# Issuing both column halves of the probability-value products behind one eviction, in a two-layer attention trunk

## The chip, the cores and the metric

The kernel is one program on one core of a Trainium2 chip. The metric is the device time of one execution in microseconds (us), the median over the timed runs. Before the change three runs took 1315.16, 1319.93 and 1320.21 us, so the median is 1319.93 us. Everything about where the time goes comes from one further execution that the hardware profiler recorded.

In the profile, PE is TensorE's matmuls, PEld its weight loads, DVE is VectorE, ACT is ScalarE, POOL is GpSimd and SP issues DMAs. A line number such as L1058 is a line of the kernel. Tile names are shown without their buffer numbers: `s_po` is a PSUM tile of the pool `po`.

## What is computed

The reference is a two-layer decoder trunk on one sequence of 512 tokens with 1024 features, in float32. Cut to what matters here:

```
layer 0: h = rmsnorm(x); q, k, v, gates = split(h @ a_w_in)
         o = gated sum of three attention branches (compressed, selected, window), 12 heads of 64, causal
         o_mem = attention of 4 heads over 256 memory tokens
         x = x + concat(o, o_mem) @ a_w_out;  x = x + relu(rmsnorm(x) @ w_up)^2 @ w_down
shared keys and values from x
layer 1: q = rmsnorm(x) @ b_w_in; dilated attention, 8 slots x 3 groups, over the shared keys and values
         o_mem as above;  x = x + concat(o, o_mem) @ b_w_out;  squared-ReLU MLP as above
```

Every attention branch ends in a product of probabilities and values, out = softmax(scores) @ v, with a head dimension of 64. These products are what the change touches.

## The kernel before

**The work.** The program runs through six stretches: a start with the first projection, the attention of layer 0 with its projections, the MLP of layer 0, the shared keys and values with the first projection of layer 1, the attention of layer 1, and the MLP of layer 1. The large projections and the MLPs are made of products of two-part numbers: `mm3` (L250) issues three matmuls for each product (L253, L254, L255).

**An item of attention** has a front and a back. The front multiplies queries and keys into a PSUM tile of the pool `ps`, takes the maximum on DVE, the exponential on ACT (recorded at L216) and scales on POOL (`pscale`, L684). The back transposes the probabilities on PE into a PSUM tile of the pool `pt` (L1039 and L1045 in layer 0, L1540 and L1549 in layer 1, L638 for the memory heads) and copies them to an SBUF tile with the tag `pt4`. This copy is called an eviction below. It is made by `evT` (L686), which gives it to DVE for some of the calls (L690) and to ACT for the rest (L692); in layer 1 all of them go to ACT. `attend` (L142) runs fronts and backs of the items with a lag of one and mixes in steps of projections that are due.

**The products of probabilities and values** come at the end of the last item of a group. Two heads share one PSUM tile `O` of the pool `po`, which has a single buffer: the first head writes the output partitions 0 to 63 and the second head 64 to 127. So each product is a matmul with only 64 columns of the array, and they are written in pairs, first head and second head in turn. Four places do this:

- L1058 in layer 0, 12 groups. Six of them (first half of the queries) have 4 pairs, with 256, 128, 256 and 128 moving columns; six (second half) have 8 pairs, for each of two branches 256, 256, 256 and 128.
- L646 for the memory heads, 4 groups of 2 pairs with 512 columns, two in layer 0 and two in layer 1.
- L1562 in layer 1, 4 groups of 4 pairs with 256, 256, 256 and 128 columns.
- L1575 in layer 1, 4 groups of 4 pairs with 128 columns.

That makes 24 groups and 224 such matmuls. Each is a float32 matmul and stands in the trace as two MATMUL records, so that a group of 4 pairs shows as x16. The first head's probabilities of a group are evicted well before the second head's; in the second half of the queries in layer 0, the two branches of the second head have an eviction each.

**What sets the order.** The program is built with a scheduler that decides the order of the instructions on each engine while the kernel is built, from its own idea of when operands are ready. On the chip each engine then takes its instructions in that fixed order, and an instruction waits on semaphores for what it needs. Since a matmul of the first head needs only the first head's evictions, the scheduler may place it ahead of its partner, with other work between the two.

Of the kernel before, what the change touches and what calls it, by code (L numbers as in the profile page):

```python
# [10 lines left out]
AF = mybir.ActivationFunctionType  # L11
# [169 lines left out]
class K:  # L181
# [428 lines left out]
    def mem_items(self, kf, qm, kk, outs, seg, need):  # L610

        nc = self.nc

        def front(h, ih):
            Sp = self.ps(self.pS, [P, 2, NMEM])
            for ii in range(2):
                i = ih * 2 + ii
                for hl in (0, 1):
                    nc.tensor.matmul(
                        Sp[:, ii, :], qm[0][h // 2][:, h % 2, i * P : (i + 1) * P], kk[0][hl][:, h, :],  # L620
                        start=hl == 0, stop=hl == 1,
                    )
            p, sm = self.soft(Sp, 2, NMEM)
            c = self.t("cr", [P, 2])
            nc.vector.reciprocal(out=c, in_=sm)
            for ii in range(2):
                self.pscale(p[:, ii, :], c[:, ii : ii + 1])
            return p

        pT = {}  # L630

        def back(h, ih, p):
            if ih == 0:
                pT[h] = self.t("pt4", [P, 2, S])
            pt = self.ps(self.pT, [P, 2, 2, P])
            for kb in range(2):
                for ii in range(2):
                    nc.tensor.transpose(pt[:, kb, ii, :], p[:, ii, kb * P : (kb + 1) * P], self.idf)  # L638
            self.evT(pT[h][:, :, ih * 256 : (ih + 1) * 256].rearrange("p k (i q) -> p k i q", q=P), pt)
            if h % 2 == 0 or ih == 0:  # L640
                return
            O = self.ps(self.pO, [P, S])
            for kb in range(2):
                for hp in range(2):
                    hh = h - 1 + hp
                    nc.tensor.matmul(  # L646
                        O[hp * 64 : hp * 64 + 64, :], kf[0][kb][1][:, hh * HD : (hh + 1) * HD], pT[hh][:, kb, :],
                        start=kb == 0, stop=kb == 1,
                    )
            oT = self.t("act", [P, 2, S], F32R)  # L650
            self.split(oT, O)
            outs.append(oT)

        return [Item(front, back, (h, ih), seg, need) for h in range(4) for ih in range(2)]

    def hilo(self, ki, src):
# [29 lines left out]
    def evT(self, dst, src):  # L686

        self.n += 1
        if self.n % self.ev == 0:
            self.nc.vector.tensor_copy(dst, src)  # L690
        else:
            self.nc.scalar.activation(dst, src, AF.Copy)  # L692

    def q_out(self, t, f, dsts, keys=None, e=None):

# [268 lines left out]
    def attn_a(self, g, ga, gt, cmp, out):  # L964


        nc = self.nc
# [58 lines left out]
        def back(pr, half, hp, ii, p):  # L1026
            v = ga[2]
            i = half * 2 + ii
# [25 lines left out]
            for br in range(2):  # L1054
                for j in range(nj):
                    o = P if j == nj - 1 else 0
                    for x in range(2):
                        nc.tensor.matmul(  # L1058
                            O[x * 64 : x * 64 + 64, q0 + o : q0 + 256], v[:, j, br, :], st[x][br][:, j, o:256],
                            start=half == 0 and br == 0 and j == 0, stop=False,  # L1060
                        )
# [5 lines left out]
        need = f"g{g}" if g else None  # L1067
        return (
            [Item(front, back, a, g, need) for a in order],
            [Item(cfront, cback, (i,), g, "cmp") for i in range(NB)],  # L1070
        )
# [397 lines left out]
    def attn_b(self, sp, q4, kv, oT, side):  # L1469

        nc = self.nc
# [84 lines left out]
        def close0():  # L1556
            vn = kv[1]
            O = self.ps(self.pO, [P, S])
            for j in (0, 2, 1, 3):
                n = min(2, NB - j) * P  # L1560
                for s in range(2):
                    nc.tensor.matmul(  # L1562
                        O[s * 64 : s * 64 + 64, j * P : j * P + n], vn[:, j, s * HD : (s + 1) * HD],
                        t0[s][:, j * 256 : j * 256 + n], start=j == 0, stop=j == NB - 1,
                    )
            a = self.t("raw", [P, S])
            nc.scalar.activation(a.rearrange("p (r u) -> p r u", r=4), self.perm(O), AF.Copy)
            acc.append(a)

        def close1():  # L1570
            vp = kv[2]
            O = self.ps(self.pO, [P, S])
            for r in range(4):
                for s in range(2):
                    nc.tensor.matmul(  # L1575
                        O[s * 64 : s * 64 + 64, r * P : (r + 1) * P], vp[:, r, s * HD : (s + 1) * HD], t1[s][:, r, :],
                        start=True, stop=True,
                    )
            side.add(self.norm_b(st0, st1, acc[0], O, oT))
# [184 lines left out]
```

## Time and profile before

| | us |
|---|---|
| median of three timed runs | 1319.93 |
| lowest and highest | 1315.16, 1320.21 |
| span of the profiled execution | 1316.2 |
| PE busy in it | 1266.8 |
| DVE, ACT, POOL busy | 860.7, 772.2, 377.6 |

The span runs from the first to the last instruction of the profiled execution. It is 3.7 us under the median of the timed runs and inside their spread. Ends of matmuls are modelled in the profile and reach a little into the next matmul, so how long a run of matmuls holds the array is read from starts: from its first start to the start of what comes next.

### The profile page before, as it was taken

What the parts mean: (1) busy time and instruction counts of PE and PEld (TensorE: products, weight loads), DVE (VectorE), ACT (ScalarE), POOL (GpSimd) and SP (SyncE); (2) the same over time, 40 slices, a digit from 0 to 9 for tenths busy, and PEclk for the clock granted to TensorE, in tenths of its full rate; (3) what the DMA queues carried; (4) which work ended last, traced back from release to release, by engine and by line L of the source; (5) the groups of instructions that cost most, each with busy time, mean ns of one, the idle gap of its engine ahead of it and who ended that gap; (6) DMA issues with size and microseconds to landing.
All of it is one profiled execution on the core that took longest, in us unless ns stands there. A gap on an engine that the chain in (4) does not pass through costs nothing.

```text
span 1316.2 us, 18557 instructions
## 1 busy us (share of the span) xinstructions
PE 1266.8 (96%) x6468; PEld 1041.7 (79%) x6468; DVE 860.7 (65%) x1597; ACT 772.2 (59%) x1699; POOL 377.6 (29%) x478
## 2 busy tenths in 40 slices
PE   9789989999999999999999989989999999999998
PEld 7768777677688888888887888877768888888887
DVE  6987767744566656566588566675665655747566
ACT  6765668674575354453557457777657545354462
POOL 4455574443240000000003679562324000000000
PEclk9899989999999999999999999999999999999999
DMA  7333222334379697796965431210338879697434
GB/s 263 120 98 106 97 97 81 63 74 113 120 245 240 219 279 219 262 247 208 290 197 165 134 79 49 67 45 9 95 120 267 232 269 225 221 280 223 154 112 160
DMA packets 61837, 215.28 MB, mean 164 GB/s; under 512 B 6736, under 2 KB 14928, under 8 KB 61232
## 3 DMA queue, kind: packets, MB, share of 16 engines
q1 hardware_dynamic: 50800, 143.72, 32.9%
q0 software_dynamic: 9344, 35.77, 13.8%
q10 hardware_dynamic: 1600, 34.61, 7.2%
q8 instruction: 51, 0.84, 0.2%
q14 instruction: 42, 0.34, 0.1%
HBM read 208.83 MB, written 72.35 MB: 214 GB/s over the span
## 4 chain that ended last, share of the span: by engine, by line
PE 81%; DVE 8%; ACT 4%; issue 2%; POOL 2%; DMA 2%; POOLq 0%; ACTq 0%; DVEq 0%
PE s_ps L253 13%; PE s_ps L254 13%; PE s_ps L255 13%; PE s_acc L253 6%; PE s_acc L254 6%; PE s_acc L255 6%; PE s_pt L253 3%; PE s_pt L254 3%; PE s_pt L255 3%; PE s_po L1058 2%; DVE s_w L248 2%; PE s_ps L1500 1%; PE s_pt L1045 1%; ACT s_p L216 1%; PE s_ps L1009 1%
## 5 line engine op out<-in xcount | busy, mean ns | idle before, releaser
L248 DVE TENSOR_TENSOR s_w<-s_st,s_w 128x1024 fp32r<-128x1024 f32 (+3 forms) x240 | 290.1, 1213 | 260.3 <-ACT s_w L246 259.8
L246 ACT ACTIVATE s_w<-s_st 128x1024 fp32r<-128x1024 f32 (+4 forms) x272 | 263.8, 973 | 188.0 <-PE s_pt L255 49.5
L253 PE MATMUL s_ps<-s_act,s_w 128*128 128x512 f32 x568 | 222.6, 394 | 1.4 <-ACT s_act L288 1.4
L254 PE MATMUL s_ps<-s_act,s_w 128*128 128x512 f32 x568 | 222.0, 391 | 0.0
L255 PE MATMUL s_ps<-s_act,s_w 128*128 128x512 f32 x568 | 221.8, 391 | 0.0
L253 PEld LDWEIGHTS s_ps<-s_act,s_w 128*128 128x128 f32 x568 | 106.8, 188 | 26.1 <-ACT s_act L288 3.1
L254 PEld LDWEIGHTS s_ps<-s_act,s_w 128*128 128x128 f32 x568 | 106.9, 188 | 22.9 <-issue 0.8
L255 PEld LDWEIGHTS s_ps<-s_act,s_w 128*128 128x128 f32 x568 | 106.9, 188 | 22.1
L253 PE MATMUL s_acc<-s_w,s_act 128*128 128x512 f32 (+3 forms) x288 | 103.8, 365 | 4.5 <-DVE s_tq L1424 2.6
L254 PE MATMUL s_acc<-s_w,s_act 128*128 128x512 f32 (+3 forms) x288 | 103.4, 361 | 2.2 <-DVE s_w L248 1.4
L216 ACT ACTIVATE s_p<-s_ps 128x512 f32<-128x512 f32 x64 | 38.2, 597 | 112.6 <-PE s_ps L255 112.6
L255 PE MATMUL s_acc<-s_w,s_act 128*128 128x512 f32 (+3 forms) x288 | 101.5, 358 | 0.0
L1128 POOL DMA_DIRECT2D sum<-in_w_db_dram x16 | 14.4, 902 | 300.0 <-ACT s_p L216 298.3
L684 POOL TENSOR_SCALAR s_p<-s_p,s_cr 128x256 f32<-128x256 f32 (+3 forms) x128 | 71.6, 581 | 73.3 <-DVE s_cr L1021 21.7
L216 ACT ACTIVATE s_p<-s_ps,s_nm 128x256 f32<-128x256 f32 (+3 forms) x128 | 65.6, 522 | 17.6 <-DVE s_nm L1000 7.5
L248 POOL TENSOR_TENSOR s_w<-s_st,s_w 128x512 fp32r<-128x512 f32 (+4 forms) x32 | 52.2, 1630 | 59.3 <-ACT s_w L246 59.2
L253 PEld LDWEIGHTS s_acc<-s_w,s_act 128*128 128x128 f32 x288 | 56.5, 196 | 12.5 <-DVE s_tq L1424 3.0
L692 ACT ACTIVATE s_pt<-s_pt 128x512 f32<-128x512 f32 (+2 forms) x97 | 50.7, 529 | 25.2 <-PE s_pt L638 12.1
L254 PEld LDWEIGHTS s_acc<-s_w,s_act 128*128 128x128 f32 x288 | 56.5, 196 | 7.3 <-DVE s_w L248 2.2
L255 PEld LDWEIGHTS s_acc<-s_w,s_act 128*128 128x128 f32 x288 | 56.3, 196 | 4.8 <-issue 0.6
L288 ACT ACTIVATE s_qk<-s_p 128x256 fp32r<-128x256 f32 (+1 forms) x96 | 46.9, 489 | 22.0 <-DVE s_p L1138 20.1
L1128 POOL DMA_DIRECT2D sum<-sum x16 | 14.1, 884 | 143.5 <-issue 45.8
(338 smaller groups left out, 2995.2 us busy)
## 6 DMA issues: line engine op xcount, KB each, us to landing
s_st<-in_w_up_dram SPq DMA_DIRECT2D x64, 512.0 KB, 4.3
s_st<-sum SPq DMA_DIRECT2D x64, 512.0 KB, 6.0
s_st<-in_w_db_dram SPq DMA_DIRECT2D x48, 512.0 KB, 4.3
sum<-in_w_db_dram POOLq DMA_DIRECT2D x16, 1024.0 KB, 13.5
sum<-sum POOLq DMA_DIRECT2D x16, 1024.0 KB, 9.8
s_st<-in_w_bq_dram SPq DMA_DIRECT2D x16, 384.0 KB, 3.2
s_st<-in_w_ag_dram SPq DMA_DIRECT2D x11, 512.0 KB, 4.5
s_st<-in_w_c_dram SPq DMA_DIRECT2D x8, 512.0 KB, 3.7
```

Of the source, the lines that this page charges most:

```text
L216: return lambda *a, **k: self.marks.append(f(*a, **k))
L246: nc.scalar.activation(w[:, 0], st, AF.Copy)
L248: e.tensor_tensor(out=w[:, 1], in0=st, in1=w[:, 0], op=ALU.subtract)
L253: mm(ps, lh[0], rh[0], start=start, stop=False, skip_group_check=again)
L254: mm(ps, lh[0], rh[1], start=False, stop=False, skip_group_check=again)
L255: mm(ps, lh[1], rh[0], start=False, stop=stop, skip_group_check=again)
L288: nc.scalar.activation(dst[:, 0], src, AF.Copy)
L684: self.nc.gpsimd.tensor_scalar(out=p, in0=p, scalar1=c, scalar2=1.0, op0=ALU.mult, op1=ALU.mult)
L692: self.nc.scalar.activation(dst, src, AF.Copy)
L1009: nc.tensor.matmul(Sp, q[:, blk], kk[hl][:, br, 0:n], start=hl == 0, stop=False)
L1058: nc.tensor.matmul(O[x * 64 : x * 64 + 64, q0 + o : q0 + 256], v[:, j, br, :], st[x][br][:, j, o:256], start=half == 0 and br == 0 and j = ...
L1128: self.behind(self.nc.gpsimd.dma_start(t[o], x, accum_op=ALU.add, max_dma_last_dim=4096))
```

## The change

`evT` keeps the eviction that it issued last in `self.turned`. A new helper `pair` issues a matmul and adds a dependency on that eviction, so that the matmul can't be placed or start before it. All four places that multiply probabilities by values call `pair` instead of `matmul`. When they are reached, the last eviction is that of the item that closes the group, which is the second head's last one. So both halves of every pair in a group depend on it, the first head's as well, and in the groups with 8 pairs also the pairs of the branch whose evictions were done earlier. Nothing else is edited. Matmuls and their sizes stay the same.

```
@@ evT
         self.n += 1
         if self.n % self.ev == 0:
-            self.nc.vector.tensor_copy(dst, src)
+            self.turned = self.nc.vector.tensor_copy(dst, src)
         else:
-            self.nc.scalar.activation(dst, src, AF.Copy)
+            self.turned = self.nc.scalar.activation(dst, src, AF.Copy)
+
+    def pair(self, *a, **k):
+
+        i = self.nc.tensor.matmul(*a, **k)
+        self.tc.add_manual_dep(
+            i.ins, self.turned.ins.name, mybir.DependencyInfo(mybir.DependencyClass.Sync, mybir.DependencyReason.DATA),
+            reason="both halves of the array together",
+        )
@@ attn_a, back (the same in mem_items, close0 and close1)
                     for x in range(2):
-                        nc.tensor.matmul(
+                        self.pair(
                             O[x * 64 : x * 64 + 64, q0 + o : q0 + 256], v[:, j, br, :], st[x][br][:, j, o:256],
                             start=half == 0 and br == 0 and j == 0, stop=False,
                         )
```

Lines of the kernel below the helper move by 8 (L1045 becomes L1053, L1009 becomes L1017), and all pair matmuls have the line of the helper, L696.

The scheduler places the instructions anew. On PE the 224 matmuls stood in 55 separate runs, with other PE work between them, and 20 of the runs were a single matmul. Now there are 24 runs, one for each group, and none is single. At the first group with 8 pairs in layer 0, `s_pt_250` is the tile with the first head's probabilities; on PE before:

```order
L254 MATMUL s_acc_1574<-s_w_1340,s_act_213 128x512
L1045 MATMUL s_pt_1281<-c_115,s_p_246_1184 128x128 x4
L1058 MATMUL s_po_1106<-s_pt_250_1212,s_x_369 64x256
L255 MATMUL s_acc_1574<-s_w_1340,s_act_213 128x512
L253 MATMUL s_acc_1574<-s_w_1363,s_act_236 128x512
```

and the same place on PE after:

```order
L253 MATMUL s_acc_1574<-s_w_1340,s_act_213 128x512
L254 MATMUL s_acc_1574<-s_w_1340,s_act_213 128x512
L1053 MATMUL s_pt_1281<-c_115,s_p_246_1184 128x128 x4
L255 MATMUL s_acc_1574<-s_w_1340,s_act_213 128x512
L253 MATMUL s_acc_1574<-s_w_1363,s_act_236 128x512
```

The single matmul between the transposes and the projection is gone from here; it now opens the group's run, further down.

The end of the third group with 8 pairs, on PE before. `s_pt_600` and `s_pt_601` are the second head's tiles of the two branches, `s_pt_566` and `s_pt_567` the first head's, and `s_pt_2528` is the PSUM tile whose eviction fills `s_pt_601`:

```order
L1045 MATMUL s_pt_2528<-c_115,s_p_598_2465 128x128 x4
L1058 MATMUL s_po_2289<-s_pt_600_2476,s_x_1430 64x256
L1058 MATMUL s_po_2289<-s_pt_566_2370,s_x_1430 64x256
...
L1058 MATMUL s_po_2289<-s_pt_567_2371,s_x_1430 64x256
L1039 MATMUL s_pt_2600<-c_115,s_p_609_2498 128x128 x2
L1009 MATMUL s_ps_2702<-s_qk_1297,s_qk_1296 128x512
L1009 MATMUL s_ps_2702<-s_qk_1298,s_qk_1296 128x512
L1010 MATMUL s_ps_2702<-cm,idr 128x128
L1058 MATMUL s_po_2289<-s_pt_601_2477,s_x_1430 64x256
L1058 MATMUL s_po_2289<-s_pt_567_2371,s_x_1430 64x256
```

and on PE after:

```order
L1053 MATMUL s_pt_2528<-c_115,s_p_598_2465 128x128 x4
L1017 MATMUL s_ps_2702<-s_qk_1297,s_qk_1296 128x512
L1017 MATMUL s_ps_2702<-s_qk_1298,s_qk_1296 128x512
L1018 MATMUL s_ps_2702<-cm,idr 128x128
L1047 MATMUL s_pt_2600<-c_115,s_p_609_2498 128x128 x2
L696 MATMUL s_po_2289<-s_pt_566_2370,s_x_1430 64x256
L696 MATMUL s_po_2289<-s_pt_600_2476,s_x_1430 64x256
...
L696 MATMUL s_po_2289<-s_pt_567_2371,s_x_1430 64x256
L696 MATMUL s_po_2289<-s_pt_601_2477,s_x_1430 64x256
```

The eight matmuls that stood between the last transposes and the last eviction's first reader have moved behind that eviction; three score matmuls and two transposes are left in between. On ACT, the eviction from `s_pt_2528` stands where it stood:

```order
L667 ACTIVATE s_qk_1932<-s_pt_2513 64x2x128
L504 ACTIVATE s_r_844_3322<-s_r_844_3322 128x4
L246 ACTIVATE s_w_3621<-s_st_3619 128x1024
L692 ACTIVATE s_pt_601_2477<-s_pt_2528 128x4x128
L216 ACTIVATE s_p_656_2672,s_su_2658<-s_ps_2665,s_nm_2669 128x384
```

These rows are of after; before, too, the weight copy of L246 stands just ahead of it on ACT.

More of the change, by code (lines that the diff above doesn't have):

```diff
@@ L1057, in back @@
                     for x in range(2):
-                        nc.tensor.matmul(
+                        self.pair(
                             O[x * 64 : x * 64 + 64, q0 + o : q0 + 256], v[:, j, br, :], st[x][br][:, j, o:256],
@@ L1561, in close0 @@
                 for s in range(2):
-                    nc.tensor.matmul(
+                    self.pair(
                         O[s * 64 : s * 64 + 64, j * P : j * P + n], vn[:, j, s * HD : (s + 1) * HD],
@@ L1574, in close1 @@
                 for s in range(2):
-                    nc.tensor.matmul(
+                    self.pair(
                         O[s * 64 : s * 64 + 64, r * P : (r + 1) * P], vp[:, r, s * HD : (s + 1) * HD], t1[s][:, r, :],
```

## The prediction

> **What bounds the kernel now.** I read the page first, then the stretches, then the pair matmuls in the timeline of PE. From the page, the span, PE's busy time and the chain that ended last:
>
> ```profile
> span 1316.2 us, 18557 instructions
> PE 1266.8 (96%) x6468; PEld 1041.7 (79%) x6468; DVE 860.7 (65%) x1597; ACT 772.2 (59%) x1699; POOL 377.6 (29%) x478
> PE 81%; DVE 8%; ACT 4%; issue 2%; POOL 2%; DMA 2%; POOLq 0%; ACTq 0%; DVEq 0%
> ```
>
> PE is busy nearly always and carries 81% of the chain. By stretches (busy us and instructions of PE, PEld, DVE, ACT, POOL, then the granted clock), the attention of layer 0, its MLP, the attention of layer 1 and the last MLP:
>
> ```profile
> 50.00:350.00 300.00, 278.07 (x1642) 218.11 (x1641) 203.60 (x502) 193.83 (x547) 149.58 (x226) 0.97 0.32 94
> 350.00:690.00 340.00, 340.00 (x1524) 281.23 (x1523) 217.41 (x311) 183.02 (x270) 28.39 (x26) 1.00 0.79 237
> 800.00:970.00 170.00, 158.59 (x1055) 131.43 (x1054) 105.63 (x239) 116.21 (x374) 85.58 (x101) 0.96 0.16 48
> 970.00:1316.20 346.20, 342.19 (x1529) 282.93 (x1527) 219.32 (x313) 180.03 (x262) 24.43 (x22) 1.00 0.70 213
> ```
>
> The MLPs have no room and no pair matmul. All that the change touches lies in the first and third row, where PE is busy 278.07 of 300 and 158.59 of 170 us: the bound, but not alone. About 33 us there are waits on other engines.
>
> **What a lone half costs.** The timeline of PE (start, length, line, xcount of records) around the single matmul of the first group with 8 pairs:
>
> ```profile
> 125.85 0.60 PE L1045 MATMUL s_pt<-c,s_p 128*128 128x128 f32 x4
> 126.39 0.65 PE L1058 MATMUL s_po<-s_pt,s_x 128*64 128x256 f32 x2
> 126.96 0.50 PE L255 MATMUL s_acc<-s_w,s_act 128*128 128x512 f32 x1
> ```
>
> The single matmul holds the array from 126.39 to 126.96, 0.57 us; its printed length is 0.08 more, so I take 0.07 off every printed length below. The rest of a group of 4 pairs, then both parts of a group of 8 pairs, then a group of 4 pairs in layer 1 that already stood together:
>
> ```profile
> 176.53 1.51 PE L1058 MATMUL s_po<-s_pt,s_x 128*64 128x256 f32 x14
> 140.95 1.73 PE L1058 MATMUL s_po<-s_pt,s_x 128*64 128x256 f32 x16
> 143.34 1.73 PE L1058 MATMUL s_po<-s_pt,s_x 128*64 128x256 f32 x14
> 893.45 1.73 PE L1562 MATMUL s_po<-s_pt,s_x 128*64 128x256 f32 x16
> ```
>
> The last row has 8 matmuls with 2 x 896 columns and takes 1.66 us, while one lone matmul with 256 columns takes 0.58. So the two halves do run beside each other. The groups of L1575, in their three parts before, and a memory group in its two:
>
> ```profile
> 860.13 0.43 PE L1575 MATMUL s_po<-s_pt,s_x 128*64 128x128 f32 x2
> 897.68 0.66 PE L1575 MATMUL s_po<-s_pt,s_x 128*64 128x128 f32 x8
> 909.75 0.65 PE L1575 MATMUL s_po<-s_pt,s_x 128*64 128x128 f32 x6
> 326.64 1.07 PE L646 MATMUL s_po<-s_pt,s_act 128*64 128x512 f32 x2
> 331.29 1.93 PE L646 MATMUL s_po<-s_pt,s_act 128*64 128x512 f32 x6
> ```
>
> From 893.45 (896 columns on each half, 1.66 us) and 897.68 (256 on each, 0.59 us) a full run costs 1.07 us for 640 columns, 1.67 ns each, and 0.16 us fixed. The lone ones obey the same line: 0.58, 0.36 and 1.00 us for 256, 128 and 512 columns. A lone half costs what a pair costs.
>
> [...]
>
> **The change part by part.** *Joined halves.* Each group by the line above, against what its parts took:
>
> - Six groups of 4 pairs in layer 0: 0.58 + 1.44 = 2.02 now; 768 columns give 0.16 + 1.28 = 1.44. Saved 0.58 each, 3.48.
> - Six groups of 8 pairs: 0.58 + 1.66 + 1.66 = 3.90 now; 1792 columns give 3.15. Saved 0.75 each, 4.50.
> - Three memory groups that stood apart (the fourth stood together): 1.00 + 1.86 = 2.86; both halves full take the 1.86 that the longer half takes now. Saved 1.00 each, 3.00.
> - Four groups of L1575: 0.36 + 0.59 + 0.58 = 1.53; 512 columns give 1.02. Saved 0.51 each, 2.04.
> - The first group of L1562, the only one apart, in three parts below: 0.58 + 0.58 + 1.23 = 2.39; together 1.66. Saved 0.73.
>
> ```profile
> 810.46 0.65 PE L1562 MATMUL s_po<-s_pt,s_x 128*64 128x256 f32 x2
> 814.86 0.65 PE L1562 MATMUL s_po<-s_pt,s_x 128*64 128x256 f32 x4
> 821.68 1.30 PE L1562 MATMUL s_po<-s_pt,s_x 128*64 128x256 f32 x10
> ```
>
> Sum 13.75 us.
>
> *Switches.* Four transposes ahead of other full-array work take 0.44 us on the chain; ahead of the single half at 126.39 they held the array from 125.85, 0.54:
>
> ```profile
> 120.18 0.44 PE s_pt L1045 x4
> ```
>
> So a run costs 0.10 us more in the instruction before it. 55 runs become 24: 31 x 0.10 = 3.1 us. Together 16.9 us of PE.
>
> *The later wait.* Every run already ended in matmuls that wait for the last eviction. New is what has to be behind it. In groups of 8 pairs, the run that stood ahead of that eviction (1.66 us of cover) moves behind it. In two of the six the order leaves over twenty PE rows as cover; four have five to eight. The third group, PE and ACT:
>
> ```profile
> 227.37 0.63 PE L1045 MATMUL s_pt<-c,s_p 128*128 128x128 f32 x4 [0.55 <-POOL s_p L684]
> 227.94 1.73 PE L1058 MATMUL s_po<-s_pt,s_x 128*64 128x256 f32 x16
> 228.34 1.06 ACT L246 ACTIVATE s_w<-s_st 128x1024 fp32r<-128x1024 f32 x1
> 229.29 0.60 ACT L692 ACTIVATE s_pt<-s_pt 128x512 f32<-128x512 f32 x1
> 229.61 0.44 PE L1039 MATMUL s_pt<-c,s_p 128*128 128x128 f32 x2
> 230.51 1.73 PE L1058 MATMUL s_po<-s_pt,s_x 128*64 128x256 f32 x14
> ```
>
> The last transposes end at 227.94, the eviction behind a weight copy at 229.89. Without the run of 8, PE has only the 0.90 us from 229.61 to 230.51 to fill 1.95: it waits 1.05 us, and the score matmuls, transposes and projections queued behind it on PE wait with it. Where ACT is free it is less. In the fourth group the eviction followed at once:
>
> ```profile
> 246.56 0.60 PE L1045 MATMUL s_pt<-c,s_p 128*128 128x128 f32 x4
> 247.20 0.60 ACT L692 ACTIVATE s_pt<-s_pt 128x512 f32<-128x512 f32 x1 [0.74 <-PE s_pt L1045]
> ```
>
> There it is done 0.64 us after the transposes (246.56 + 0.60 to 247.80), within the cover. So four groups cost between 0 and 1.05 each, 0 to 4.2 us. I take 1.6, nearer the free ACT, and 0.4 for one group of 4 pairs that loses three score matmuls as cover: 2.0. In layer 1 and the memory groups the cover stays or grows, or loses one projection matmul; zero there.
>
> PE's path becomes 16.9 - 2.0 = 14.9 us shorter. DVE, ACT, POOL and SP get no instruction more or less, only other places in line: on POOL weight copies of L248 move past scalings of L684 and parts of the rotary step, on SP one weight load moves two places ahead, on ACT evictions and exponentials trade places. I set this at nothing, since PE has most of the chain; what it may cost or bring is in the rivals on both sides.
>
> *What reaches the end.* Of the 20 lone runs, 12 stand in the chain of waits; the first, at a lower clock, and the last:
>
> ```profile
> 74.90 1.05 PE s_po L1058 x2
> 962.76 1.00 PE s_po L646 x2
> ```
>
> For the other eight, PE waited for something else soon after, so time saved there turns into a longer wait. I take 12/20: 14.9 x 0.6 = 8.9 us. All of it would be 14.9; a quarter, if other chains close up as soon as PE is quicker, 3.7. The span goes from 1316.2 to 1307.3. The timed median is 3.7 us above the span, and I carry the difference over: 1319.9 - 8.9 = 1311.0 us.
>
> **The rivals.** Measurements of this kernel tell apart about 0.5%, 6.6 us: below 1313.3 is faster, above 1326.5 slower.
>
> *Other chains close up.* DVE, ACT and POOL are busy 204, 194 and 150 of the 300 us of layer 0 and feed the softmax loop. If they set the pace once PE is shorter, a quarter stays: 1319.9 - 3.7 = 1316.2. For it: 33 us of waits in these stretches. Against it: PE's 81%. Chance 0.23.
>
> *All of it arrives,* since the whole order moves up: 1319.9 - 14.9 = 1305.0. For it: PE has 96%. Chance 0.12.
>
> *Slower: the wait ahead of every run.* Where a group has no cover at all, before already shows it, a group of 4 pairs right behind its transposes:
>
> ```profile
> 98.31 1.51 PE L1058 MATMUL s_po<-s_pt,s_x 128*64 128x256 f32 x14 [1.22 <-DVE s_pt L690]
> ```
>
> If evictions come later on the chip than the order was planned for, so that all 24 runs wait 1.22 us, that is 29.3 us against 16.9 saved: 1332.3. It breaks even at 0.70 us a run and is slower by 0.5% from 0.98. Against it: the order leaves most groups the cover that they had. Chance 0.10.
>
> *The clock drops more often.* After a stretch with PE busy 5.87 of 6.80 us the granted clock fell to half, and the run in it took 3.26 us instead of 1.73:
>
> ```profile
> 913.70:920.50 6.80, 5.87 (x46) 4.89 (x45) 4.60 (x15) 6.08 (x22) 2.69 (x4) 1.00 0.00 0
> 920.50:927.40 6.90, 6.67 (x32) 4.44 (x32) 3.71 (x5) 5.08 (x18) 2.82 (x4) 0.51 0.02 5
> 922.16 3.26 PE L1562 MATMUL s_po<-s_pt,s_x 128*64 128x256 f32 x16
> ```
>
> The change takes work out of PE where it is least busy. One more such stretch costs 6.9 x 0.49 = 3.4 us; two cost 6.8: 1317.8. Chance 0.06. [...]
>
> *It doesn't do what it says,* pairs in series: only switches, (3.1 - 2.0) x 0.6 = 0.7: 1319.2. The rows above speak against it. [...] Chance 0.02.
>
> **How the numbers follow.** The forecast has the rest, 0.47. Its own bounds: 0.45 of 14.9 is 6.7, and with the waits at 0 and 0.8 of 16.9 reaching the end 13.5, so 1306.4 to 1313.2, all faster. Faster 0.47 + 0.12 = 0.59, same 0.23 + 0.06 + 0.02 = 0.31, slower 0.10. The range 1304 to 1319 takes in the forecast, most of the full gain, both small gains and the clock; it leaves out the slower case and the tails.
>
> **What would show it.** Right: the pair matmuls at L696 in 24 runs; runs of x16 in layer 0 at 1.44 us to the next start and x32 at 3.15; PE busy some 12 to 17 us less in the two attention stretches, MLP stretches unchanged; waits of PE for ACT or DVE ahead of L696 of about 2 us more in sum than before's. Wrong in the size: PE's busy time falls as said but its idle time in the two stretches grows by more than half of it (other chains), or the granted clock there falls under 0.96. Wrong in the mechanism: x32 takes over 3.9 us, or PE's waits ahead of L696 sum to over 17 us.

## The result and the profile after

| | before | after |
|---|---|---|
| median, us (first 6 executions each) | 1317.65 | 1302.66 |
| lowest and highest | 1313.27, 1320.21 | 1296.79, 1305.59 |
| ratio, with its 95% interval | | 0.9895 [0.9872, 0.9919] |
| the same once more (19 and 6 executions) | 1316.33 | 1300.82, ratio 0.9891 [0.9861, 0.9922] |
| profiled execution: time, span, mean granted clock | 1318.0, 1316.2, 0.983 | 1296.8, 1295.0, 0.995 |

The change makes the kernel 1.1% faster. The profiled execution of after was the fastest of its six, with the highest granted clock, so the 21 us between the two spans are more than the change brings. The page of after, its span, busy times and chain:

```profile
span 1295.0 us, 18552 instructions
PE 1239.9 (96%) x6468; PEld 1026.0 (79%) x6468; DVE 858.9 (66%) x1597; ACT 770.5 (59%) x1699; POOL 380.9 (29%) x478
PE 67%; DVE 5%; ACT 4%; DMA 2%; POOL 2%; issue 2%; SPq 0%; POOLq 0%; ACTq 0%; DVEq 0%
```

PE is busy 26.9 us less than before (1266.8), and idle 5.7 us more: 1295.0 - 1239.9 = 55.1 against 1316.2 - 1266.8 = 49.4. The 26.9 us are not all joined runs: before's profiled execution ran 44 us of its span at half clock, that of after 14. The stretches that the prediction read, in after (the same columns as there):

```profile
50.00:350.00 300.00, 271.02 (x1678) 215.57 (x1677) 209.21 (x512) 199.40 (x556) 154.43 (x228) 0.99 0.35 99
350.00:690.00 340.00, 339.85 (x1528) 281.41 (x1526) 217.67 (x320) 186.22 (x282) 25.72 (x24) 1.00 0.82 242
800.00:970.00 170.00, 160.11 (x1083) 133.36 (x1083) 115.60 (x243) 119.75 (x364) 78.88 (x92) 1.00 0.23 68
```

The MLP stretch is as full as before. In layer 0's attention the same 300 us hold 271.02 us of PE instead of 278.07, and ACT, DVE and POOL do more in them: the work moved up. For the same reason the prediction's sign of 12 to 17 us less PE in the two attention stretches can't be read from windows of fixed length, since later work moves into them. In layer 1's attention the clock is 1.00 where it was 0.96.

The joined groups, in the timeline of PE (start, length, line, xcount). First a group of 8 pairs and what follows it, then a group of 4 pairs:

```profile
140.02 3.25 PE L696 MATMUL s_po<-s_pt,s_x 128*64 128x256 f32 x32
143.20 0.53 PE L717 MATMUL s_pt<-idr,s_qki 128*128 128x128 f32 x4
...
173.40 1.52 PE L696 MATMUL s_po<-s_pt,s_x 128*64 128x256 f32 x16
174.85 0.36 PE L727 MATMUL s_pt<-idr,s_qki 128*128 128x128 f32 x2
```

From start to next start they hold the array 3.18 and 1.45 us, where 3.15 and 1.44 were forecast. The other kinds came out at 1.87 (memory), 1.67 (L1562 of before) and 1.02 us (L1575 of before), within 0.01 us of the forecast.

The third group with 8 pairs, where the prediction worked out a wait of 1.05 us, on PE and ACT:

```profile
221.09 0.41 PE L1047 MATMUL s_pt<-c,s_p 128*128 128x128 f32 x2
222.71 3.25 PE L696 MATMUL s_po<-s_pt,s_x 128*64 128x256 f32 x32 [1.21 <-ACT s_pt L692]
...
221.13 1.04 ACT L246 ACTIVATE s_w<-s_st 128x1024 fp32r<-128x1024 f32 x1
222.08 0.58 ACT L692 ACTIVATE s_pt<-s_pt 128x512 f32<-128x512 f32 x1
```

PE waits 1.21 us for the eviction that stands behind the weight copy on ACT. All waits ahead of pair matmuls sum to 4.0 us in after and 2.4 us in before, 1.7 us more; 2.0 were forecast.

PE's waits ahead of score and pair matmuls in layer 0's attention (150 to 310 us; us in total, times, longest), before and after:

```profile
PE s_ps L1009 <- ACT s_p L216: 1.9, 6, 0.6
PE s_ps L619 <- ACT s_p L216: 0.5, 1, 0.5
PE s_po L1058 <- ACT s_pt L692: 0.4, 2, 0.2
```

```profile
PE s_ps L1017 <- ACT s_p L216: 4.2, 8, 1.2
PE s_po L696 <- ACT s_pt L692: 2.0, 4, 1.2
PE s_ps L619 <- ACT s_p L216: 1.5, 1, 1.5
```

L1009 and L1017 are the same score matmuls, and what they wait for is ACT making exponentials (L216). These three kinds of waits grew by 4.9 us, while all of PE's idle time there grew by 6.0. They are the waits in which the saved time shows up; e13 below asks whether ACT is its cause.

### The profile page after: what moved, and what is told of

Its sections match the earlier page's. It is cut to its first block, busy times and chain, and to the rows that moved or that the text cites. A ratio compares the mean times of both kernels' runs of the same rounds, so it can differ in the third digit from the quotient of the medians.

```text
span 1295.0 us, 18552 instructions
## 1 busy us (share of the span) xinstructions
PE 1239.9 (96%) x6468; PEld 1026.0 (79%) x6468; DVE 858.9 (66%) x1597; ACT 770.5 (59%) x1699; POOL 380.9 (29%) x478
## 4 chain that ended last, share of the span: by engine, by line
PE 67%; DVE 5%; ACT 4%; DMA 2%; POOL 2%; issue 2%; SPq 0%; POOLq 0%; ACTq 0%; DVEq 0%
PE s_ps L253 13%; PE s_ps L254 13%; PE s_ps L255 13%; PE s_acc L254 3%; PE s_acc L255 3%; PE s_acc L253 3%; PE s_pt L254 3%; PE s_pt L255 3%; PE s_pt L253 3%; PE s_po L696 2%; DVE s_w L248 1%; ACT s_p L216 1%; PE s_ps L1508 1%; ACT s_w L246 1%; DVE s_pt L216 1%
## 5 line engine op out<-in xcount | busy, mean ns | idle before, releaser
L248 DVE TENSOR_TENSOR s_w<-s_st,s_w 128x1024 fp32r<-128x1024 f32 (+3 forms) x240 | 287.1, 1200 | 256.7 <-ACT s_w L246 255.5
L246 ACT ACTIVATE s_w<-s_st 128x1024 fp32r<-128x1024 f32 (+4 forms) x272 | 263.8, 973 | 186.2 <-PE s_pt L255 44.0
L216 ACT ACTIVATE s_p<-s_ps 128x512 f32<-128x512 f32 x64 | 38.2, 597 | 112.6 <-PE s_ps L255 112.6
L254 PE MATMUL s_acc<-s_w,s_act 128*128 128x512 f32 (+3 forms) x288 | 101.6, 354 | 3.1 <-POOL s_w L248 1.7
L253 PE MATMUL s_acc<-s_w,s_act 128*128 128x512 f32 (+3 forms) x288 | 101.3, 357 | 2.7 <-DVE s_tq L912 1.1
L1136 POOL DMA_DIRECT2D sum<-in_w_db_dram x16 | 14.4, 901 | 301.7 <-ACT s_p L216 300.0
L255 PE MATMUL s_acc<-s_w,s_act 128*128 128x512 f32 (+3 forms) x288 | 99.8, 351 | 0.0
L216 ACT ACTIVATE s_p<-s_ps,s_nm 128x256 f32<-128x256 f32 (+3 forms) x128 | 65.5, 522 | 16.3 <-DVE s_nm L1008 7.0
L248 POOL TENSOR_TENSOR s_w<-s_st,s_w 128x512 fp32r<-128x512 f32 (+4 forms) x32 | 55.4, 1732 | 50.0 <-ACT s_w L246 41.4
L253 PEld LDWEIGHTS s_acc<-s_w,s_act 128*128 128x128 f32 x288 | 54.5, 190 | 9.6 <-DVE s_tq L912 1.2
L254 PEld LDWEIGHTS s_acc<-s_w,s_act 128*128 128x128 f32 x288 | 54.7, 190 | 8.3 <-POOL s_w L248 2.3
L255 PEld LDWEIGHTS s_acc<-s_w,s_act 128*128 128x128 f32 x288 | 54.6, 190 | 4.0
```

What stands on the lines that cost most here:

```text
L216: return lambda *a, **k: self.marks.append(f(*a, **k))
L246: nc.scalar.activation(w[:, 0], st, AF.Copy)
L248: e.tensor_tensor(out=w[:, 1], in0=st, in1=w[:, 0], op=ALU.subtract)
L253: mm(ps, lh[0], rh[0], start=start, stop=False, skip_group_check=again)
L254: mm(ps, lh[0], rh[1], start=False, stop=False, skip_group_check=again)
L255: mm(ps, lh[1], rh[0], start=False, stop=stop, skip_group_check=again)
```

## The experiments

Each kernel was timed beside the kernel before on the same chip, in five rounds. Executions of one kernel differ by up to 1.2%, and the time falls as the mean granted clock of the execution rises: one line for all 252 executions of these kernels (one of e8, at a clock of 0.936, is left out) falls by 0.93 us for each 0.001 of clock and leaves a scatter of 2.0 us. So two numbers stand for each kernel: the measured ratio, and the time that this line gives at a clock of 0.987, which is before's mean over 101 executions. At that clock before itself comes to 1314.5 to 1315.4 us on the four chips of the later runs.

| kernel | median us | ratio to before [95%] | mean clock | us at 0.987 |
|---|---|---|---|---|
| before (101 executions) | 1315.35 | 1 | 0.9870 | 1315.1 |
| after (twice 6) | 1302.66, 1300.82 | 0.9895, 0.9891 | 0.9905 | 1304.8 |
| e1 layer 0's attention alone | 1314.15 | 0.9984 [0.9969, 0.9999] | 0.9860 | 1312.8 |
| e2 memory heads and layer 1 alone | 1306.20 | 0.9911 [0.9883, 0.9939] | 0.9892 | 1307.2 |
| e5 memory heads alone | 1312.65 | 0.9975 [0.9956, 0.9993] | 0.9867 | 1312.5 |
| e6 layer 1 alone | 1307.10 | 0.9934 [0.9911, 0.9957] | 0.9905 | 1310.6 |
| e9 all but groups of 8 pairs | 1305.12 | 0.9926 [0.9898, 0.9954] | 0.9908 | 1309.2 |
| e12 groups of 8 pairs alone | 1311.41 | 0.9970 [0.9952, 0.9987] | 0.9874 | 1312.3 |
| e3 second head shifted by one | 1303.80 | 0.9908 [0.9884, 0.9932] | 0.9887 | 1305.7 |
| e11 halves apart | 1327.84 | 1.0082 [1.0054, 1.0110] | 0.9872 | 1326.5 |
| e4 wait by branch | 1308.00 | 0.9936 [0.9911, 0.9961] | 0.9870 | 1307.8 |
| e7 10.3 us of PE more, layer 0 | 1322.15 | 1.0043 [1.0018, 1.0069] | 0.9863 | 1320.7 |
| e8 10.3 us of PE more, the rest | 1318.78 | 1.0022 [1.0006, 1.0037] | 0.9858 | 1317.3 |
| e13 after, evictions to DVE | 1309.64 | 0.9976 [0.9948, 1.0003] | 0.9859 | 1308.7 |
| e14 before, evictions to DVE | 1317.33 | 1.0034 [1.0017, 1.0051] | 0.9860 | 1316.0 |
| e16 a wait filled | 1305.39 | 0.9940 [0.9919, 0.9961] | 0.9869 | 1305.0 |

The last column is uncertain by about 0.6 to 0.8 us for each kernel, 0.2 for before.

**The change in two parts.** In e1 only L1066 (L1058 of before) keeps `pair`, in e2 only the other three places do:

```diff
-                        self.pair(
+                        nc.tensor.matmul(
                             O[x * 64 : x * 64 + 64, q0 + o : q0 + 256], v[:, j, br, :], st[x][br][:, j, o:256],
```

Shown is e2's edit.

> Only the products of layer 0's attention wait for the last eviction; memory heads and layer 1 are as before (37 runs of pair matmuls where before has 55 and after 24). PE time saved by the terms of the prediction: 3.48 + 4.50 for the joined halves, 18 runs less at 0.10 = 1.8, later waits 2.0, net 7.8 us. Theory A (nearly all PE time saved reaches the end): 7 to 8 us under before, ratio 0.9940 to 0.9947. Theory B (the share of 0.6 was right, the rest of the gain of after is a granted clock that fell less often): 4.7 us plus what the clock brings, which shows as fewer us at half clock; at before's clock a ratio of 0.9964. Theory C (the new order is better by luck elsewhere, not through the pairs): no relation to 7.8; ratio anywhere from 0.990 to 1.000, and this one and the other half of the change don't add up to the whole.

> The other part alone: memory heads and layer 1 wait for the last eviction, layer 0's attention is as before (42 runs). PE time saved by the terms of the prediction: 3.00 + 2.04 + 0.73 for the joined halves, 13 runs less at 0.10 = 1.3, no later wait, net 7.1 us. Theory A: 6.5 to 7.1 us under before, ratio 0.9946 to 0.9951. Theory B: 4.3 us, ratio 0.9967, plus a difference of clock. Theory C: no relation to 7.1; the two parts don't add up to the 13.8 us of the whole.

At the same clock e1 is 2.3 us under before and e2 7.9, together 10.2; after is 10.3 under it. The parts add up, so theory C falls. After against e2 and against e1 gives the same two parts, 2.4 and 8.0. But A and B fall too, since the parts don't share one rate: of 7.8 us layer 0 keeps 2.3, and of 7.1 us the rest keeps all. PE's busy time between 155 and 310 us (the columns of the stretches), in before, e1 and after:

```profile
155.00:310.00 155.00, 144.66 (x919) 112.94 (x918) 100.71 (x286) 109.30 (x333) 78.12 (x119) 0.98 0.29 75
```

```profile
155.00:310.00 155.00, 138.70 (x920) 110.76 (x919) 101.72 (x290) 109.75 (x335) 79.93 (x122) 0.98 0.29 77
```

```profile
155.00:310.00 155.00, 138.65 (x940) 110.05 (x940) 101.78 (x288) 112.83 (x345) 80.80 (x122) 1.00 0.32 83
```

In e1 PE issues as many records there as before (920 and 919), does them in 6 us less and is idle 6 us more (16.3 of 155 us against 10.3). After is as idle, with 940 records. What DVE, ACT and POOL got done in that stretch grew by only 0.4 to 2.3% in e1.

**Each place by itself.** e5 keeps `pair` at L646 alone, e6 at L1570 and L1583 alone.

> Only the products of the memory heads wait for the last eviction (4 groups); 52 runs. Theory D (new, after the first four runs: what a saved us of PE is worth differs by stage; in layer 0's attention about 0.3 arrives, since PE then waits for ACT and POOL, in the memory heads and layer 1 all of it; and the new order also removes the wait of 2.4 us on POOL's scaling at the end of layer 1's attention, with the half-clock stretch of 3.4 us that follows it): 3.0 + 3 x 0.10 of PE, 2.0 of the wait, up to 1.7 of the clock: 5.3 to 7.0 us under before, ratio 0.9947 to 0.9960, no PE wait over 1 us ahead of the last memory transposes, and a mean clock about 0.001 higher. Theory E (every saved us of PE arrives to about the same share, 0.75, and the rest is chance of order and clock): 2.5 us, ratio 0.998.

> Only the two places in layer 1 (8 groups) wait for the last eviction; 45 runs. PE saves 2.04 + 0.73 + 10 x 0.10 = 3.8 us. Theory D: all of it, 3.8 us under before, ratio 0.997, with the wait of 2.4 us at the end still there. Theory E: 2.8 us, ratio 0.998. With the memory heads alone this should add up to the 0.9911 of both.

By ratio e5 is 3.3 us faster and e6 8.7. At the same clock it is 2.6 and 4.5, for 3.3 and 3.8 us of PE that were worked out. Together that is 7.1 for 7.1, so the two are worth about what PE saves; e5 alone, at 2.6, is as near to theory E's 2.5. Theory D was wrong in the wait and in where the clock comes in: the wait of 2.4 us is gone from e5's trace, but neither the 2.0 us nor the clock that it was to bring came with it, and e6 has the higher clock.

**Groups of 4 and of 8 pairs.** Both edits are on L1066, where `half` is 1 in groups of 8 pairs; in e12 the three other places are as before.

```diff
-                        self.pair(
+                        (nc.tensor.matmul if half else self.pair)(
```

> As after, but the six groups with 8 pairs in layer 0 don't wait for the last eviction (36 runs; they stand as lone, 8 and 7 pairs as before). Theory G (the 6 us by which PE's idle time between 155 and 310 us grew, from 10.2 to 16.2, comes with the joined groups of 8 pairs, whose 3.2 us in one piece hold up the score matmuls and with them ACT): idle time there stays near 10 to 11 us, the groups of 4 pairs bring 3.5 + 0.6 whole, and against the run with memory heads and layer 1 alone (0.9911) it is 4 us faster: ratio 0.988, 1 to 2 us under after. Theory H (any shortening of PE in layer 0 turns into waits on ACT and POOL, whichever groups): idle time grows by 2 to 3 us, ratio 0.9895 to 0.991.

> The six groups with 8 pairs alone wait for the last eviction, all else is as before (42 runs). PE saves 4.5 for the joined halves and 1.2 for 12 runs. Theory G: idle time of PE between 155 and 310 us is about 16 us as in after, the 5.7 us are all given back, ratio 0.999 to 1.001. Theory H: a third to a half arrives, 2 to 3 us, ratio 0.998.

The same stretch in e9 and in e12:

```profile
155.00:310.00 155.00, 140.64 (x902) 110.38 (x901) 98.49 (x284) 107.32 (x329) 75.94 (x118) 0.97 0.27 71
```

```profile
155.00:310.00 155.00, 141.61 (x933) 111.79 (x932) 103.61 (x296) 110.61 (x338) 80.67 (x122) 1.00 0.30 76
```

Idle time there is 14.4 us in e9 and 13.4 in e12, against 10.3 in before. By the prediction's terms the groups of 4 pairs save 4.1 us of PE, and PE idles 4.1 us more; at the same clock e9 is 2.0 us slower than e2, which lacks them, and the two times leave 1.2 us of doubt. (e9's stretch also holds fewer records than before's, 902 for 919, and ran at a lower clock.) The groups of 8 pairs save 5.7, PE idles 3.1 more, and 2.8 us arrive at the same clock. So theory G, which laid the idle time on the long runs of 8 pairs, falls: whichever group is shortened in layer 0, much of it turns into waits, as theory H has it.

**Lone halves inside a run.** e3 issues the second head's matmul one pair later, e11 all of the first head's first. The order around the runs is nearly after's in e3.

```diff
+def skewed(js, by=1):
+    js = list(js)
+    n = len(js)
+    return [p for i in range(n + by) for p in ([(js[i], 0)] if i < n else []) + ([(js[i - by], 1)] if i >= by else [])]
...
-                for j in range(nj):
...
-                    for x in range(2):
+            for (br, j), x in skewed([(br, j) for br in range(2) for j in range(nj)]):
```

(In e11, `by` is the length of the list.)

> All of the change, but in each group the second head's matmul is issued one pair later (first, first, second, first, second, ..., second), so that each group opens and closes with a lone half. 24 runs, waits and the order around them are nearly those of after. Each group gets longer by one slot: 256 columns (0.43 us) in 16 groups, 512 (0.86) in 4, 128 (0.21) in 4, sum 11.2 us; if the two halves of a shifted pair also wait for the longer of the two, 13.7 us. Theory A: 10 to 13.7 us more than after, ratio to before 0.997 to 1.000. Theory B: 0.6 of it, 6.7 to 8.2 us more, ratio 0.9946 to 0.9957. Theory C: nearly as after, 0.9895 to 0.992.

> As after, but in each group all matmuls of the first head are issued before all of the second head's. In the run with a shift by one pair each group took only 0.05 us longer, so a waiting half let the other half pass it. If PE looks far ahead, a group again costs nothing more and the time is after's (ratio 0.990). If it looks ahead by one matmul or two, most of a group runs in series: its columns count twice, 1.28 us more for 4 pairs, 2.99 for 8, 1.71 for a memory group, 1.50 and 0.85 in layer 1, sum 41.8 us, so 35 to 45 us more than after (ratio 1.016 to 1.024).

As a dose for the theories e3 said nothing, since the shift cost almost nothing. A group of 4 pairs in e3, then in e11:

```profile
178.78 1.57 PE L702 MATMUL s_po<-s_pt,s_x 128*64 128x256 f32 x16
180.28 0.36 PE L733 MATMUL s_pt<-idr,s_qki 128*128 128x128 f32 x2
```

```profile
177.12 2.22 PE L702 MATMUL s_po<-s_pt,s_x 128*64 128x256 f32 x16
179.27 0.36 PE L733 MATMUL s_pt<-idr,s_qki 128*128 128x128 f32 x2
```

1.50 us in e3 against 1.45 in after, and 2.15 in e11. A group of 8 pairs took 3.23 in e3 and 5.61 in e11, a memory group 1.87 in both. Over all groups e11's runs are 24 us longer than after's, and it is 21.7 us slower at the same clock: about nine tenths of this PE time arrives. The 35 to 45 us that were worked out for a short reach did not come, since the first head's last matmuls still run beside the second head's first ones (in a group of 4 pairs the second head starts at 0.71 of 2.15 us). Of the 24 us, 18.8 lie in layer 0's attention (0.70 for each group of 4 pairs, 2.43 for each of 8). So PE time that is added there arrives nearly whole, where of saved PE time a quarter did.

**The wait at the third group of 8 pairs.** In e4 the pairs of a branch depend on that branch's own last eviction:

```diff
                     self.evT(st[hp][br][:, 0 : i + 1, ii * P : (ii + 1) * P], pt)
+                    st["ev", br] = self.turned
...
-                            start=half == 0 and br == 0 and j == 0, stop=False,
+                            start=half == 0 and br == 0 and j == 0, stop=False, to=half and st["ev", br],
```

> As after, but in the groups with 8 pairs the pairs of a branch wait only for that branch's own last eviction, so that four pairs can again fill the time until the last eviction, now with both halves together. 29 runs for 24: 5 x 0.10 = 0.5 us more. Taken away: the wait of 1.21 us ahead of the third of these groups, and up to 0.8 us ahead of the others. Theory A (PE time counts nearly whole): 1 to 1.5 us less than after, ratio 0.988 to 0.989. Theory B: 0.6 to 0.9 us less, not to be told from after. Theory C: a new order, 0.985 to 0.995.

At the place it did what it should: the third group starts without a wait, and the second memory group's last matmul starts at 337.0 us against 338.5 in after. But the order in layer 1 moved as well, and PE there waits 1.1 us for an eviction (L1642, L1640 in after) for which in after it waits at most 0.3. In all e4 is 3.0 us slower than after at the same clock, and its clock is lower (0.9870 for 0.9905). So the gain of 1.5 us in one place was lost elsewhere; that the order lost it is likely, but not shown.

**Work added.** e7 computes the first pair of each group of 4 four times more, e8 does the same amount in the other 12 groups. The group's own matmuls write the same places afterwards.

```diff
+            for x in 4 * [0, 1] if half == 0 else []:
+                self.pair(O[x * 64 : x * 64 + 64, 0:256], v[:, 0, 0, :], st[x][0][:, 0, 0:256], start=True, stop=True)
```

> As after, with PE work added in layer 0's attention: ahead of each of the six groups with 4 pairs, the first pair (256 columns) is computed four times more and overwritten. 24 pairs of 0.43 us, 10.3 us of PE. Theory D: about 0.3 of it arrives, 3 us more than after (ratio to before 0.992), and PE's idle time between 160 and 310 us falls by about 6 us. Theory E: 0.75 to 1, 8 to 10 us more than after, ratio 0.996 to 0.997.

> As after, with the same 10.3 us of PE added in the other 12 groups instead: one pair of 512 columns more in each memory group, two of 256 and four of 128 columns more in the groups of layer 1. Theory D: all of it arrives, 10 us more than after, ratio to before 0.997. Theory E: 0.75 of it, 8 us more, 0.9955, and the same as for the dose in layer 0.

Both theories were wrong. At the same clock e7 is 15.9 us slower than after and e8 12.5, both more than the 10.3 us of PE. PE between 155 and 310 us in e7:

```profile
155.00:310.00 155.00, 139.80 (x973) 109.89 (x972) 99.75 (x285) 105.52 (x321) 77.21 (x116) 1.00 0.27 70
```

Its idle time there is 15.2 us, hardly less than after's 16.3: added work did not fill the waits that saved work had opened. Part of it is order: e7 has e4's order in layer 1, which in e4 cost about 3 us. How much of the rest is order was not separated.

**Evictions from ACT to DVE.** One number is changed, in after (e13) and in before (e14):

```diff
-        self.ev = 3
+        self.ev = 2
```

> As after, but in layer 0 every second eviction by the count goes to DVE instead of every third (8 of some 100 rows move from ACT to DVE, the order moves with them). Theory H (PE time saved in layer 0 is lost in waits on ACT: 4.2 us ahead of the score matmuls and 2.0 us ahead of the pair matmuls): the waits on ACT there fall by 2 us or more and the time by 1 to 4 us: ratio 0.986 to 0.989. Rival (it is the length of the whole softmax chain, not ACT's load): waits only change their name, ratio 0.989 to 0.992.

> The kernel before with the same move of evictions, as a control: without the joined groups PE waits for ACT less (1.9 us ahead of the score matmuls, 0.4 ahead of the pair matmuls), so under theory H it should bring less than in after, 0 to 1 us: ratio 0.999 to 1.001.

The waits of the score matmuls in e13, 150 to 310 us:

```profile
PE s_ps L1017 <- ACT s_p L216: 2.7, 7, 0.6
```

They fell from 4.2 to 2.7 us, and those of the pair matmuls on ACT, 2.0 us in after, are no longer among the largest. Yet e13 is 3.9 us slower than after at the same clock and e14 0.9 slower than before. So a lighter ACT shortens these waits but not the kernel. That ACT's load alone is the limit there is not supported; which other place took the time was not found.

**The granted clock.** The unaltered kernel was run again for its clock, and one wait was filled with useless matmuls.

> The changed kernel once more, unaltered, for its granted clock over more executions. Theory D1 (the change itself raises the granted clock, by joining the groups of layer 1): mean clock 0.990, that of before 0.9865; time 1302 to 1303, ratio 0.9895. Theory F (the higher clock in the first six runs was chance): mean clock within 0.001 of before's, time 1304 to 1306, ratio 0.991 to 0.992.

The mean clock was 0.9907 and the time 1300.8 us. With the first six, twelve executions have 0.9905 against 0.9870: theory D1 holds in that the higher clock was no chance. In layer 1's attention PE's order is exactly after's in e2, e6 and e9 and nearly so in e3; it is exactly before's in e1 and e14 and nearly so in e5 and e12. The kernels with after's order have 0.9887 to 0.9908 (after, e2, e3, e6, e9), those with before's 0.9860 to 0.9874 (before, e1, e5, e12, e14). The kernels were sorted so after their clocks were known. The rest, e4, e7, e8, e11, e13 and e16, in which layer 1's order or its runs are others than after's, have 0.9858 to 0.9872. So the mean clock goes with the order in layer 1, and joining its groups raised it only together with the order that after has there.

What makes the clock fall at one place can be seen in stretches of 3.41 us. In every trace the granted clock changes only on a grid of that length. Two grid cells of before that hold the longest waits of PE, each with the cell behind it (us, busy us of PE, PEld, DVE, ACT, POOL, granted clock):

```profile
43.33:46.74 3.41, 1.07 (x8) 0.71 (x6) 3.41 (x15) 2.50 (x9) 1.04 (x1) 1.00 0.45 154
46.74:50.15 3.41, 3.41 (x14) 3.28 (x14) 3.41 (x15) 1.89 (x7) 0.00 (x0) 0.50 0.02 5
954.69:958.10 3.41, 1.03 (x6) 0.35 (x3) 2.70 (x4) 1.60 (x4) 3.41 (x3) 1.00 0.19 48
958.10:961.51 3.41, 3.41 (x11) 2.74 (x11) 0.00 (x0) 0.60 (x1) 1.93 (x4) 0.50 0.19 51
```

PE was busy 1.07 and 1.03 of 3.41 us, and in the next cell the clock was half. After has the first of these waits too, 2.33 us long and ending at 46.31, but there the grid cuts it in two:

```profile
41.71:45.12 3.41, 2.27 (x12) 1.89 (x11) 3.41 (x13) 1.19 (x4) 2.21 (x3) 1.00 0.46 130
45.12:48.53 3.41, 2.22 (x15) 2.20 (x16) 3.41 (x16) 3.09 (x12) 0.10 (x1) 1.00 0.09 29
48.53:51.94 3.41, 3.41 (x23) 3.31 (x22) 3.41 (x12) 1.25 (x5) 1.40 (x2) 1.00 0.00 0
```

PE is busy 2.27 and 2.22 of 3.41 us in the two cells, and the clock stays whole. Over the 17 traces, 127 half-clock stretches began inside the programs. Counted by how busy PE was in a cell at full clock, the next cell was at half clock behind all 60 cells with PE busy under 0.4 of the cell, behind 39 of 74 with 0.4 to 0.6, 27 of 331 with 0.6 to 0.8, and 1 of 5864 above. So in these traces PE's busy time in a cell goes with most of the falls of the clock, but does not settle them all.

In after the wait of 2.34 us at 758.50 fell into one cell, and the next one was half:

```profile
755.09:758.50 3.41, 1.07 (x8) 0.76 (x6) 3.41 (x3) 0.96 (x3) 3.41 (x3) 1.00 0.08 20
758.50:761.91 3.41, 3.41 (x14) 3.41 (x15) 3.06 (x4) 1.74 (x4) 3.33 (x4) 0.50 0.76 245
```

e16 fills this wait (`fill` is 10 for the first call in layer 1):

```diff
         self.hilo(qi, t)
+        if self.fill:
+            n, self.fill = self.fill, 0
+            O = self.pO.tile([P, nh, HD], F32, name=f"fill_{n}", tag="po")
+            for _ in range(n):
+                nc.tensor.matmul(O, self.idr, qi[:, :, 0, :], start=True, stop=True)
```

> As after, with ten matmuls of 384 columns, whose output nobody reads, in the one wait of 2.34 us ahead of the first rotated queries of layer 1, at about 758 us. They read what ACT wrote for these queries, so they start when that is done and end before DVE's part is. Theory J (the clock falls to half when PE was idle for about half of a stretch of 3.41 us): no half-clock stretch within 4 us of that place, where 12 of 13 profiled executions of these kernels had one or two; the queries' transposes start no later. Time 1 to 2 us less if nothing else moves, but the order behind it moves too, so the time decides nothing; the trace at that place does. Rival (the clock falls for another reason, such as the load of the chip at that point): the stretch is still there.

The filled wait, and the grid cells around it in e16:

```profile
763.20 1.93 PE L716 MATMUL fill<-s_qki,idr 128*128 128x384 f32 x10
765.72 0.70 PE L723 MATMUL s_pt<-idr,s_qki 128*128 128x128 f32 x6 [0.58 <-DVE s_qki L661]
```

```profile
760.96:764.38 3.42, 3.42 (x21) 3.42 (x21) 2.53 (x2) 2.29 (x6) 3.42 (x3) 1.00 0.01 2
764.38:767.79 3.41, 2.83 (x20) 2.50 (x19) 3.41 (x5) 1.47 (x4) 3.41 (x3) 1.00 0.66 230
767.79:771.20 3.41, 3.41 (x22) 3.37 (x21) 1.85 (x5) 1.25 (x4) 3.25 (x5) 1.00 0.69 188
```

The clock stays whole, as theory J has it, but this run does not decide it: the grid cuts the filled wait at 764.38. Without the fill PE would have been busy about 2.4 of 3.42 us in one cell and 2.1 of 3.41 in the next (an estimate from the rows above), and behind cells with 0.6 to 0.8 half clock came in 27 of 331 cases. The time, 1305.4 us, was no better than after's; in its trace other waits of PE are longer than in after, two of them 2.0 us behind 790 us.

The other 16 traces decide it. In each of them PE waits 2.33 or 2.34 us at this place, unfilled, and only the wait's place on the grid differs. In 13 of them one cell there has PE busy 1.65 us or less, and the next cell is at half clock (12 of the 14 executions that there were when the expectation named 12 of 13). In the other three (e11, e12, e13) the grid cuts the wait so that PE is busy at least 1.79 us in both cells, and the clock stays whole. So at this place the wait is what the clock falls for, and whether it falls goes with how the wait lies on the grid.

What raises the mean clock is a further question. The longest waits in before's layer 1 (830 to 970 us), and in after's (820 to 950):

```profile
PE s_acc L253 <- DVE s_tq L1424: 2.6, 2, 1.9
PE s_pt L638 <- POOL s_p L684: 2.4, 1, 2.4
```

```profile
PE s_pt L1557 <- ACT s_pt L692: 1.2, 2, 0.6
PE s_pt L717 <- ACT s_pt L692: 1.0, 2, 0.5
PE s_acc L254 <- POOL s_w L248: 1.0, 1, 1.0
```

Waits of 1.9 and 2.4 us have become waits of at most 1.0. It would be a simple cause, but the other kernels do not bear it out. The traces of e4, e7, e8 and e13 have no PE wait over 1.5 us behind 800 us either, and their mean clocks are 0.9858 to 0.9870. The trace of e6 has one of 2.1 us there, and its mean clock is 0.9905. One trace is also only one place on the grid: of the stretch from 810 to 970 us, e6's ran 13.7 us at half clock, as much as before's, and both of after's none. So what in after's order raises the mean clock stays open.

## Why the prediction was right and wrong

- **Joined halves: right.** Every kind of run came out within 0.03 us of its forecast, so the lone halves cost what was said. The measured runs against their parts in before give 13.5 us for the 13.75 forecast. Its rival of pairs in series did not come: 1792 columns on each half took 3.18 us.
- **The switches: right.** The 0.10 us were read from one place. Over the 45 runs of before that start without a wait at full clock, the instruction ahead held the array 0.09 us longer than others of its shape.
- **The later wait: right in place and size.** 1.21 us at the third group for 1.05, and 1.7 in sum for 2.0.
- **"What reaches the end": the step that failed.** It carried PE's 14.9 us to the end with one share, on a base from three executions and with the clock left as it was. All three terms were off, and all in one direction; together they put the measured 1302.66 below the range's 1304.
- **Its share: near in total, by luck.** One share, 12/20, was taken for all lone runs, from whether they stood in the chain of one execution. At the same clock 10.3 of the 16.9 us of PE arrive, a share of 0.61. Its parts show that the share was wrong: 2.3 of 9.8 us in layer 0, 7.9 of 7.1 elsewhere. The rival "other chains close up" describes layer 0, and "all of it arrives" the rest. The count itself had it: of the lone runs 5 of 12 stood in the chain in layer 0's attention, and 7 of 8 elsewhere. Because the share was taken of 14.9, net of the waits, the forecast of 8.9 was 1.4 us short.
- **Its clock: only half considered.** The sum put the clock's change at nothing, and the rivals had only a clock that "drops more often". It dropped less often: 0.9905 for 0.9870, at 0.93 us for each 0.001 another 3.3 us. The prediction thought of PE as less busy, and not of where its waits would lie.
- **Its base: a wrong carry.** The forecast set out from 1319.93, a median of three, and carried the 3.7 us over the span along as if they belonged to the kernel. The time outside the span is 1.7 or 1.8 us in every execution, and the rest is scatter: over 101 executions before has 1315.35. That alone put the forecast 4.6 us too high.
- So 1311.0 against 1302.66 is 4.6 of base, 1.4 of share and 3.3 of clock, less about 1 by which those six executions lie over the mean of twelve.
- **The slower rival**, 1.22 us ahead of every run, did not come: waits ahead of the joined runs sum to 4.0 us over all 24, not 29.3.

## What to carry to other kernels

A microsecond of PE had a price by stage here. In layer 0, where other engines feed PE in a loop, a quarter of what was saved arrived (2.3 of 9.8 us), though work added there cost nearly its full time or more (e11 about nine tenths, e7 15.9 us for 10.3); in the other stages all of what was saved arrived (7.9 us for 7.1). Count by stage before applying a share, and take the base from many executions. And a wait had two prices here, its length and, where it left PE busy under 0.4 of one 3.41 us cell, a half clock in the next (behind all 60 such cells). No run here turned the second price into time by itself: e16, which filled one such wait, was no faster than after.

## What the runs showed of the hardware that was not expected

**Two halves passed each other.** In e3's group of 4 pairs the first head's second matmul (128 columns) is issued ahead of the second head's first (256 columns). A record does not say which head it is of, but the columns tell: of the first four records, all of 256 columns, two must be the second head's, since the first head's second matmul has 128. The first ten records of the group at 178.78 us, start in ns from the run's first and moving columns:

```
0 256   14 256   267 256   280 256   483 128   496 128   592 128   649 128   701 256   758 256
```

The second head's first matmul starts at 14 ns, and the one issued ahead of it, which needs the same half as the running one, at 483. So in this group the order of issue is not the order of starts: a waiting matmul of one half was passed by one of the other half. In e11 the reach was one waiting matmul: with four of the first head issued first, the second head starts at 706 ns, when the first head's third has started (701) and only its fourth is left waiting, and the run takes 2.15 us for 1.45. With two of each (memory groups, 1.87 us in e11 and in after) nothing is lost.

**A lone half was dear only where no other half was near.** e3's shifted pairs open and close a run with a lone half by the order of issue, and yet a run costs 0.05 us more: as the records show, the other half's matmul passes and starts beside the first. The lone half of before has full-array work on both sides, and it costs 0.58 us for 256 columns, as much as 256 columns on both halves (0.59).
